# Junction to the first MLP product of a diffusion block: weight splits one step ahead of token sums, weight rows in freed pages, early pairs interleaved

## The chip, the cores and the metric

One core of a Trainium2 chip runs one transformer-like block over 1024 tokens of 1024 channels. The metric is the device time of one execution in microseconds (us), the median of three runs. Engines: PE is TensorE (matmuls; PEld its weight loads), DVE is VectorE, ACT is ScalarE, POOL is GpSimd, SP issues the DMA transfers. Work runs on an engine in the order of its own instruction list; engines wait for each other by semaphores.

## The reference

The part around the change: the residual stream x (1024 tokens) gets its mixing branch, is normalised, scaled and shifted, and goes through a squared-ReLU MLP with D_FF = 4096.

```
x = x + gt1 * branch_merge(...)            # ends in "merged @ w_out", 1024x1024
x = x + gt2 * sq_relu_mlp(modulate(rms_norm(x, g_mlp), sh2, sc2), w1, w2)

def sq_relu_mlp(h, w1, w2):
    return jnp.square(jax.nn.relu(h @ w1)) @ w2
```

gt2 is a vector that a product of the conditioning vector with a 1024x6144 matrix gives.

## The kernel before

**Number format.** A float32 operand is split into a high part (a ScalarE copy to fp32r, a 32-bit format in which PE multiplies in one pass) and a low part (a VectorE subtraction, source minus high part). Both stand in `split` (L98), so nearly every split has line L98. A product then takes three passes: high x high, high x low, low x high. One product of the first MLP multiplication is twelve matmuls of 128x128 by 128x512 (four contraction tiles, three passes), in `mm` (L958).

**Seven products in place of eight.** h @ w1 is cut into 16 `Pair`s n. A pair covers 256 columns of w1 (two arrays of 128x1024 that a weight load brings) and both halves of the contraction and of the tokens, as 2x2 blocks. Strassen-Winograd sums give it seven products: p1 (a11 b11), p2 (a12 b21, added in the same PSUM bank A), p6 (s2 t2, bank B), p5 (s1 t1, bank C), p7 (s3 t3, added in B), p4 (a22 t4, added in B) and p3 (s4 b22, added in C). Weight sums s1 to s4 are made per pair (`sums13`, `sums24`, `s12`, `s34`); token sums t1 to t4 once, for four contraction tiles k. Products that add to one bank have VectorE or ScalarE reading the bank between them: p1 is copied (L967) before p2 adds to A, `p6` is read (L977) before p7 adds to B, p7 is read (L986, L987) before p4 adds to B.

**What comes before.** The projection `out_mm` (L859) makes merged @ w_out in two column halves dh, eight token tiles i each. Two tiles share one PSUM tile of two banks, and the second waits until VectorE has read the first (L893). `norm_tile` normalises a token tile when its second half is done: a square with accumulation on ScalarE (L217), a square root (L211), reciprocal and scaling on VectorE (L212, L813, gives xn[i]). The first four tiles are transposed and modulated in `norm_half0`; the last four in `norm_half1(k)`, k = 0 to 3, which is the junction. `gv.reduce()` makes gt2's row with fp32 matmuls against a vector of ones (L296), read by VectorE (L297).

**One step k of the junction in before.** PE transposes eight 128x128 blocks (L819); ScalarE evacuates them with scale and shift (L823) into b12 and b22; GpSimd makes t3 = b22 - b12 (L842), VectorE t1 = b12 - b11 (L843) and t2 = b22 - t1 (L844), GpSimd t4 = b21 - t2 (L845). Then b22, (t1, t2) and (t3, t4) are split, each by a ScalarE copy and a VectorE subtraction. Behind that `early_top` loads a11 and a12 of pair k+1 into one of four 4 KB work buffers (`wr_tile`) and splits them; p1 and p2 of pairs 0 to 3 are computed between the steps. p6(0) then needs t2 of all k.

**What sets the order.** PE, DVE and ACT are under a manual schedule here: their lists have the order of the code. Before that, in the projection, a scheduler places instructions by priority, and fills a wait of PE with matmuls of the next tile. SP and GpSimd follow the same program. Tiles are taken from pools with a fixed number of slots (24 pages of 4 KB in `pg`, 17 in `yp`, four work buffers); a tile that takes a used slot waits for the slot's last readers.

Of the kernel before, what the change touches and what calls it, by code (L numbers as in the profile page):

```python
# [24 lines left out]
P = 128  # L25
# [6 lines left out]
HB = 512  # L32
# [18 lines left out]
def block_kernel(es: ExitStack, tc: tile.TileContext, a, out):  # L51
# [27 lines left out]
    def page(shape, dt=F32, pool=None, tag="s"):  # L79
        return (pool or pg).tile(shape, dt, tag=tag, name=nm("pg"))  # L80
# [10 lines left out]
    def wr_tile():  # L91
        return wp.tile([P, 1024], F32, tag="wr", name=nm("wr"))
# [654 lines left out]
    with tc.tile_pool(name="yp", bufs=17, reuse_waits="tile") as yp:  # L747
# [89 lines left out]
        def norm_half1(k):  # L837
# [7 lines left out]
            G.tensor_tensor(t34[:, 1], b21, t12[:, 1], ALU.subtract)  # L845
            t = page([P, 2, HB], F32R)
# [52 lines left out]
        gv.reduce()  # L899
# [6 lines left out]
        class Pair:  # L906
# [7 lines left out]

            def early_top(self, new):

                r = wr_tile()
                dma(r, a["w1"][2 * self.n])
                self.put(r, ("a11", "a12"), new([P, 2 * HB], F32R), new([P, 2 * HB], F32R))
# [261 lines left out]
        with tc.manual_schedule(engines={mybir.EngineType.PE, mybir.EngineType.DVE, mybir.EngineType.Activation}):  # L1181
            pr[0].p1()
            norm_half1(0)
            pr[1].early_top(page)
            pr[0].p2()
            pr[1].p1()
            norm_half1(1)
            pr[2].early_top(page)
            pr[1].p2()
            pr[2].p1()  # L1190
            norm_half1(2)
            pr[3].early_top(ypage)
            pr[2].p2()
            pr[3].p1(ypage)
            norm_half1(3)
            pr[3].p2()
            pr[1].load()
            pr[1].sums13()
            for n in range(NP):
                c, nx, early = pr[n], pr[n + 1] if n + 1 < NP else None, n < NE  # L1200
                if not early:
                    c.p1()
                if n > NE:
                    pr[n - 1].out4()
                c.p6()
# [5 lines left out]
                if nx:  # L1211
                    nx.s12()
                else:
                    c.f2 = page([P, T])
                    mlp2.begin()
                c.p7()
                if early:
                    if n + 1 == NE:
                        nx.top()
                    else:  # L1220
                        nx.s34()
                        nx.last()
                    c.p4()
                    c.p3()
                    c.out4()
                    if n + 1 == NE:
                        c.out3()
                else:
                    c.p2()
                    if nx:  # L1230
                        nx.top()
                    c.p3()
                    c.out3()
# [120 lines left out]
```

## Time and profile before

| | us |
|---|---|
| median of 3 runs (lowest, highest) | 1449.17 (1448.98, 1449.18) |
| profiled execution | 1448.78 |
| its span, first to last instruction | 1447.0 |
| PE busy | 1385.9 |
| DVE busy | 1045.1 |
| ACT busy | 605.3 |
| start of p1(0), and of p5(0) behind p6(0), on PE | 776.98, 829.8 |

The profiled execution takes 1.8 us more than its span and lies 0.39 us under the median. PE is the engine whose work fills the span; the other engines matter where PE waits for them. Times on the axis below count from the span's start. The mean granted clock of the span is 0.992 of full speed.

### The profile page before, as it was taken

To read this page: it belongs to the slowest core of one execution; us is meant where nothing else is said; L and a number is where in the kernel's file an instruction comes from. 1 tells how busy PE (TensorE), PEld (TensorE's weight loads), DVE (VectorE), ACT (ScalarE), POOL (GpSimd) and SP (SyncE) were. 2 spreads that over 40 slices of the span, in tenths; PEclk is the share of its full clock that TensorE was granted. 3 is DMA by queue.
4 is the path that set the end of the run, shared out by engine and by line. 5 is a ranking of instruction groups with operands and counts; after the bars stand their busy time and mean duration, and the time that the engine had idled before them with its cause. 6 is when DMAs were issued, how large, how long until landed. Compare 5 with 4: busy or idle time off the path is not lost. (4 is left out here: it accounts for less than half of the span.)

```text
span 1447.0 us, 16245 instructions
## 1 busy us (share of the span) xinstructions
PE 1385.9 (96%) x6352; PEld 1128.9 (78%) x6352; DVE 1045.1 (72%) x1254; ACT 605.3 (42%) x747; POOL 13.0 (1%) x14
## 2 busy tenths in 40 slices
PE   4999999999999999999997799999999999999996
PEld 3888888778888878788875577888887888888885
DVE  7664647789888987844746676666664987969958
ACT  7452337654765577412134422222222544333412
POOL 0000000000000000000000200000000000000000
PEclk9999999999999999999999899999999999999998
DMA  8532712342234225547712142333326562340332
GB/s 331 191 117 68 273 38 73 120 146 84 90 121 148 74 86 177 167 143 246 268 73 102 57 147 102 116 117 117 117 73 219 217 212 72 122 147 1 111 137 102
DMA packets 64556, 192.57 MB, mean 133 GB/s; under 512 B 7203, under 2 KB 7611, under 8 KB 64479
## 3 DMA queue, kind: packets, MB, share of 16 engines
q1 hardware_dynamic: 64479, 191.53, 38.2%
q8 instruction: 50, 0.82, 0.2%
q14 instruction: 27, 0.22, 0.0%
HBM read 154.27 MB, written 37.23 MB: 132 GB/s over the span
## 5 line engine op out<-in xcount | busy, mean ns | idle before, releaser
L321 PE MATMUL mm<-pg,wh 128*128 128x512 f32 x1120 | 308.4, 396 | 0.5 <-DVE pg L98 0.5
L321 PEld LDWEIGHTS mm<-pg,wh 128*128 128x128 f32 x1120 | 204.6, 189 | 43.7 <-DVE pg L98 1.0
L958 PE MATMUL bk<-pg,wh 128*128 128x512 f32 x720 | 225.9, 395 | 1.9 <-DVE wr L297 1.1
L321 PE MATMUL mm<-pg,wl 128*128 128x512 f32 x560 | 175.4, 394 | 0.0
L958 PEld LDWEIGHTS bk<-pg,wh 128*128 128x128 f32 x720 | 135.0, 188 | 34.5 <-DVE wr L297 2.1
L958 PE MATMUL bk<-pg,wl 128*128 128x512 f32 x360 | 141.6, 393 | 0.0
L98 DVE TENSOR_TENSOR wl<-wr,wh 128x1024 fp32r<-128x1024 f32 (+2 forms) x73 | 81.5, 1119 | 76.6 <-ACT wh L98 76.5
L98 ACT ACTIVATE wh<-wr 128x1024 fp32r<-128x1024 f32 (+2 forms) x73 | 71.0, 975 | 147.9 <-PE mm L321 67.0
L321 PEld LDWEIGHTS mm<-pg,wl 128*128 128x128 f32 x560 | 105.4, 188 | 24.3
L98 ACT ACTIVATE wh<-pg 128x1024 fp32r<-128x1024 f32 (+1 forms) x52 | 52.4, 1027 | 141.0 <-PE bk L958 52.7
L98 ACT ACTIVATE pg<-pg 128x1024 fp32r<-128x1024 f32 (+4 forms) x90 | 76.3, 878 | 44.2 <-DMA pg<-act_d 12.6
L859 PE MATMUL mm<-pg,pg 128*128 128x512 f32 x384 | 91.9, 397 | 0.0
L958 PE MATMUL bk<-pg,pg 128*128 128x512 f32 x264 | 71.1, 419 | 19.7 <-ACT pg L98 15.1
L98 DVE TENSOR_TENSOR pg<-pg,pg 128x1024 fp32r<-128x1024 f32 (+4 forms) x79 | 73.8, 969 | 18.0 <-ACT pg L98 17.9
L859 PEld LDWEIGHTS mm<-pg,pg 128*128 128x128 f32 x384 | 71.0, 188 | 17.8 <-DVE g L893 2.2
L958 PEld LDWEIGHTS bk<-pg,wl 128*128 128x128 f32 x360 | 67.6, 188 | 15.9
L958 PEld LDWEIGHTS bk<-pg,pg 128*128 128x128 f32 x264 | 51.9, 201 | 35.9 <-ACT pg L98 19.0
L98 DVE TENSOR_TENSOR wl<-pg,wh 128x1024 fp32r<-128x1024 f32 (+1 forms) x52 | 60.2, 1178 | 22.9 <-ACT wh L98 22.9
L1094 PE MATMUL mm<-pg,pg 128*128 128x512 f32 x240 | 74.1, 390 | 0.0
L776 PE MATMUL mm<-pg,wh 128*128 128x512 f32 x256 | 70.0, 394 | 1.7 <-ACT pg L98 1.7
L1108 DVE TENSOR_TENSOR pg<-pg,mm 128x1024 f32<-128x1024 f32 x34 | 41.0, 1218 | 39.4 <-PE mm L1094 38.3
L1094 PE MATMUL mm<-pg 128*128 128x512 f32 x164 | 64.1, 391 | 0.0
(281 smaller groups left out, 2457.2 us busy)
## 6 DMA issues: line engine op xcount, KB each, us to landing
wr<-in_win SPq DMA_DIRECT2D x36, 512.0 KB, 4.4
wr<-in_w SPq DMA_DIRECT2D x35, 512.0 KB, 3.5
pg<-act_d SPq DMA_DIRECT2D x70, 256.0 KB, 4.9
pg<-in_wm SPq DMA_DIRECT2D x32, 512.0 KB, 8.2
wr<-in_wm SPq DMA_DIRECT2D x32, 512.0 KB, 3.8
act_d<-pg SPq DMA_DIRECT2D x32, 512.0 KB, 3.0
pg<-in_w SPq DMA_DIRECT2D x56, 256.0 KB, 5.4
pg<-in_x SPq DMA_DIRECT2D x16, 512.0 KB, 8.2
```

Of the source, the lines that this page charges most:

```text
L98: return S.activation(hi, src, AF.Copy), V.tensor_tensor(lo, src, f32(hi), ALU.subtract)
L321: PE.matmul(ps[:, h * HB:(h + 1) * HB], l[:, k, :], r[:, h * HB:(h + 1) * HB], start=k == 0 and i == 0, stop=k == KT - 1 and i == 2)
L776: PE.matmul(ps[:, h * HB:(h + 1) * HB], l[:, k, :], r[:, h * HB:(h + 1) * HB], start=k == 0 and i == 0, stop=k == KT - 1 and i == 2)
L859: PE.matmul(ps, l, r, start=k == 0 and j == 0, stop=k == KT - 1 and j == 2)
L958: PE.matmul(ps, l, r, start=first and k == 0 and i == 0, stop=k == 3 and i == 2, skip_group_check=not first)
L1094: PE.matmul(t[j], l, r, start=u not in self.ON and k == 0 and n == 0, stop=k == len(op) - 1 and n == 2, skip_group_check=u in self.ON)
L1108: V.tensor_tensor(t, t, ps, ALU.subtract if u in self.SUB else ALU.add)
```

## The change

1. `gv.reduce()` moves from behind the whole projection to between its two halves.
2. `early_top` is cut in two: `early_load` loads the upper weight rows of a pair into a page of `pg` (before: a work buffer), `early_top` splits them. The load and split of pair 1 come ahead of p1(0); those of pairs 2 and 3 come between the token sums and the splits of steps 0 and 1.
3. `norm_half1` is cut into `half1_sums` (transposes, evacuation, t1 to t4) and `half1_split` (the splits).
4. In pairs 0 to 2, p6 of the next pair stands between p7 and p4; in pair 3, the top split of pair 4 comes ahead of p7 and p1 of pair 4 stands between p7 and p4.

```diff
@@ -834,7 +834,7 @@
                     split(hf[k][:, j], t[:, 0], t[:, 1])
                     tb[("b11", "b21")[j]][k] = (t[:, 0], t[:, 1])
 
-        def norm_half1(k):
+        def half1_sums(k):
             g, t12, t34 = ypage([P, 2, HB]), *(wr_tile().rearrange("p (a b) -> p a b", b=HB) for _ in range(2))
             for j in range(2):
                 norm_block(k + 4 * j, 1, g[:, j], False, bank())
@@ -843,6 +843,9 @@
             V.tensor_tensor(t12[:, 0], b12, b11, ALU.subtract)
             V.tensor_tensor(t12[:, 1], b22, t12[:, 0], ALU.subtract)
             G.tensor_tensor(t34[:, 1], b21, t12[:, 1], ALU.subtract)
+            return b22, t12, t34
+
+        def half1_split(k, b22, t12, t34):
             t = page([P, 2, HB], F32R)
             split(b22, t[:, 0], t[:, 1])
             tb["b22"][k] = (t[:, 0], t[:, 1])
@@ -896,7 +899,8 @@
                     norm_tile(i)
                     if i == 3:
                         norm_half0()
-        gv.reduce()
+            if dh == 0:
+                gv.reduce()
         gt2 = const.tile([P, D], F32, tag="gt", name="gt2")
         dma(gt2, gt_d[1].partition_broadcast(P))
 
@@ -912,11 +916,13 @@
                 for j, r in enumerate(self.r):
                     dma(r, a["w1"][2 * self.n + j])
 
+            def early_load(self):
+
+                self.r0 = page([P, 2 * HB])
+                dma(self.r0, a["w1"][2 * self.n])
+
             def early_top(self, new):
-
-                r = wr_tile()
-                dma(r, a["w1"][2 * self.n])
-                self.put(r, ("a11", "a12"), new([P, 2 * HB], F32R), new([P, 2 * HB], F32R))
+                self.put(self.r0, ("a11", "a12"), new([P, 2 * HB], F32R), new([P, 2 * HB], F32R))
 
             def put(self, src, names, hi, lo):
                 split(src, hi, lo)
@@ -1179,30 +1185,37 @@
             pr[0].last()
         psum_pool("banks", 8)
         with tc.manual_schedule(engines={mybir.EngineType.PE, mybir.EngineType.DVE, mybir.EngineType.Activation}):
+            pr[1].early_load()
+            pr[1].early_top(page)
             pr[0].p1()
-            norm_half1(0)
-            pr[1].early_top(page)
+            h1 = half1_sums(0)
+            pr[2].early_load()
+            pr[2].early_top(page)
+            half1_split(0, *h1)
             pr[0].p2()
             pr[1].p1()
-            norm_half1(1)
-            pr[2].early_top(page)
+            h1 = half1_sums(1)
+            pr[3].early_load()
+            pr[3].early_top(ypage)
+            half1_split(1, *h1)
             pr[1].p2()
             pr[2].p1()
-            norm_half1(2)
-            pr[3].early_top(ypage)
+            h1 = half1_sums(2)
+            half1_split(2, *h1)
             pr[2].p2()
             pr[3].p1(ypage)
-            norm_half1(3)
+            h1 = half1_sums(3)
+            pr[1].load()
+            half1_split(3, *h1)
+            pr[1].sums13()
             pr[3].p2()
-            pr[1].load()
-            pr[1].sums13()
             for n in range(NP):
                 c, nx, early = pr[n], pr[n + 1] if n + 1 < NP else None, n < NE
-                if not early:
+                if n > NE:
                     c.p1()
-                if n > NE:
                     pr[n - 1].out4()
-                c.p6()
+                if n == 0 or not early:
+                    c.p6()
                 if n and early:
                     pr[n - 1].out3()
                 if nx:
@@ -1213,13 +1226,16 @@
                 else:
                     c.f2 = page([P, T])
                     mlp2.begin()
+                if n + 1 == NE:
+                    nx.top()
                 c.p7()
                 if early:
-                    if n + 1 == NE:
-                        nx.top()
-                    else:
+                    if n + 1 < NE:
+                        nx.p6()
                         nx.s34()
                         nx.last()
+                    else:
+                        nx.p1()
                     c.p4()
                     c.p3()
                     c.out4()
```

How this moves the engines' lists, at three places. Lines of the file after are higher by 3 to 6 from L885 on: L859 becomes L862, L958 L964, L967 L973, L971 L977, L977 L983, L986 L992, L987 L993, L993 L999, L1000 L1006, L1004 L1010.

**PE, from the last matmuls of token tile 6 of the second projection half to the first of tile 7.** mm_5793 and mm_5802 are the PSUM tile that both share, smp the gate's bank. Before:

```order
L859 MATMUL mm_5793<-pg_5497,pg_5177 128x512 x2
L859 MATMUL mm_5793<-pg_5497,pg_5178 128x512
L296 MATMUL smp_5866<-gacc,ones 1x512
L859 MATMUL mm_5793<-pg_5304,pg_4761 128x512 x2
L859 MATMUL mm_5793<-pg_5304,pg_4762 128x512
```

After:

```order
L862 MATMUL mm_5802<-pg_5497,pg_5177 128x512 x2
L862 MATMUL mm_5802<-pg_5497,pg_5178 128x512
L862 MATMUL mm_5802<-pg_5304,pg_4761 128x512 x2
L862 MATMUL mm_5802<-pg_5304,pg_4762 128x512
L862 MATMUL mm_5802<-pg_5339,pg_4771 128x512 x2
```

The L296 matmul between the tiles is gone; in the list after the two of them stand ahead of and behind the last tile of the first half.

**ACT, from step 0's evacuation to step 1's.** pg_5922 (after: pg_5928) holds b12, b22 of step 0; wr_5923, wr_5924 (wr_5929, wr_5930) its sums; bk_5907 and bk_5971 (bk_5913, bk_5977) are bank A of pairs 0 and 1. Before:

```order
L823 ACTIVATE pg_5922<-bk_5931,mod 128x512
L98 ACTIVATE pg_5941<-pg_5922 128x512
L98 ACTIVATE pg_5944<-wr_5923 128x1024
L98 ACTIVATE pg_5948<-wr_5924 128x1024
L98 ACTIVATE pg_5954<-wr_5952 128x1024
L971 ACTIVATE pg_5920<-bk_5907 128x512
L967 ACTIVATE pg_5984<-bk_5971 128x512
L823 ACTIVATE pg_5986<-bk_5989,mod 128x512
L823 ACTIVATE pg_5986<-bk_5995,mod 128x512
```

After:

```order
L823 ACTIVATE pg_5928<-bk_5937,mod 128x512
L98 ACTIVATE wh_5890<-pg_5884 128x1024
L98 ACTIVATE wh_5894<-pg_5885 128x1024
L98 ACTIVATE pg_5949<-pg_5947 128x1024
L98 ACTIVATE pg_5953<-pg_5928 128x512
L98 ACTIVATE pg_5956<-wr_5929 128x1024
L98 ACTIVATE pg_5960<-wr_5930 128x1024
L977 ACTIVATE pg_5926<-bk_5913 128x512
L973 ACTIVATE pg_5990<-bk_5977 128x512
L823 ACTIVATE pg_5992<-bk_5995,mod 128x512
```

The copy of weights of pair 1 (pg_5954 from wr_5952) that stood behind step 0's three splits is gone from here (it is made ahead of p1(0)); pair 2's (pg_5949 from pg_5947) stands ahead of them. Behind them the order is as before: relu of p2(0), copy of p1(1), evacuation of step 1.

**DVE, around p7 of pair 2.** bk_6350 (after: bk_6308) is bank B of pair 2, bk_6402 bank B of pair 3 after. Before:

```order
L98 TENSOR_TENSOR wl_6384<-pg_6346,wh_6383 128x1024
L986 TENSOR_TENSOR pg_6387<-pg_6048,bk_6350 128x512
L987 TENSOR_TENSOR pg_6387<-pg_6387,bk_6370 128x512
L98 TENSOR_TENSOR wl_6403<-pg_6347,wh_6402 128x1024
L98 TENSOR_TENSOR pg_6406<-wr_6343,pg_6406 128x512
L993 TENSOR_TENSOR pg_6387<-pg_6048,bk_6350 128x512
L1004 SCALAR_TENSOR_TENSOR pg_6387<-pg_6387 128x1024
```

After:

```order
L98 TENSOR_TENSOR wl_6384<-pg_6361,wh_6383 128x1024
L992 TENSOR_TENSOR pg_6387<-pg_6054,bk_6308 128x512
L993 TENSOR_TENSOR pg_6387<-pg_6387,bk_6370 128x512
L983 TENSOR_TENSOR pg_6403<-pg_6112,bk_6402 128x512
L98 TENSOR_TENSOR wl_6418<-pg_6362,wh_6417 128x1024
L98 TENSOR_TENSOR pg_6421<-wr_6358,pg_6421 128x512
L999 TENSOR_TENSOR pg_6387<-pg_6054,bk_6308 128x512
L1010 SCALAR_TENSOR_TENSOR pg_6387<-pg_6387 128x1024
```

Between the two reads of bank B behind p7 (L992, L993) and the split of s3, s4 stands now the read of the next pair's p6 (L983).

## Rows read from the trace of the kernel before

**Rows 1.** Page, part 1: busy time, share of the span, instructions.

```profile
PE 1385.9 (96%) x6352; PEld 1128.9 (78%) x6352; DVE 1045.1 (72%) x1254; ACT 605.3 (42%) x747; POOL 13.0 (1%) x14
```

**Rows 2.** Waits of PE, whole span: who waited for whom, us in total, times, longest.

```profile
PE bk L958 <- ACT pg L98: 15.1, 3, 7.2
...
PE bk L958 <- DVE pg L986: 3.4, 4, 0.9
...
PE bk L958 <- DVE wr L297: 1.1, 1, 1.1
```

**Rows 3.** One window of the junction: busy us of each engine, PEclk, DMA, GB/s.

```profile
800.00:810.00 10.00, 5.67 (x21) 4.38 (x22) 4.44 (x4) 4.34 (x6) 1.52 (x1) 0.83 0.17 52
```

**Rows 4.** Timeline of PE: start, us, line, op, tiles, count, idle before.

```profile
768.10 1.02 PE L296 MATMUL smp<-gacc,ones 128*1 128x512 f32 x2
...
774.82 1.02 PE L296 MATMUL smp<-gacc,ones 128*1 128x512 f32 x2
...
779.88 1.04 PE L819 MATMUL bk<-ident,pg 128*128 128x128 f32 x8
...
790.98 1.22 PE L958 MATMUL bk<-pg,pg 128*128 128x512 f32 x2 [7.19 <-ACT pg L98]
792.42 3.48 PE L958 MATMUL bk<-pg,pg 128*128 128x512 f32 x10 [0.23 <-DVE pg L98]
...
796.59 3.06 PE L958 MATMUL bk<-pg,pg 128*128 128x512 f32 x12
...
805.06 3.94 PE L958 MATMUL bk<-pg,pg 128*128 128x512 f32 x10 [0.71 <-DVE pg L98]
...
829.21 0.50 PE L958 MATMUL bk<-pg,wh 128*128 128x512 f32 x1 [0.79 <-DVE pg L98]
...
836.26 3.05 PE L958 MATMUL bk<-pg,pg 128*128 128x512 f32 x12 [0.78 <-DVE pg L986]
```

**Rows 5.** Timeline of ScalarE (ACT), junction.

```profile
788.92 2.00 ACT L98 ACTIVATE pg<-wr 128x1024 fp32r<-128x1024 f32 x2 [0.67 <-POOL wr L845]
...
795.94 0.60 ACT L967 ACTIVATE pg<-bk 128x512 f32<-128x512 f32 x1 [4.54 <-PE bk L958]
796.43 1.44 ACT L823 ACTIVATE pg<-bk,mod 128x512 f32<-128x512 f32 x2
...
809.04 0.60 ACT L967 ACTIVATE pg<-bk 128x512 f32<-128x512 f32 x1 [5.00 <-PE bk L958]
```

**Rows 6.** Timeline of VectorE (DVE), junction.

```profile
763.14 0.75 DVE L813 TENSOR_SCALAR pg<-pg,tiny 128x1024 f32<-128x1024 f32 x1
...
772.60 1.42 DVE L813 TENSOR_SCALAR pg<-pg,tiny 128x1024 f32<-128x1024 f32 x2 [1.26 <-PE mm L859]
...
778.09 0.75 DVE L813 TENSOR_SCALAR pg<-pg,tiny 128x1024 f32<-128x1024 f32 x1
...
782.33 2.36 DVE L98 TENSOR_TENSOR wl<-pg,wh 128x1024 fp32r<-128x1024 f32 x2 [0.48 <-ACT wh L98]
...
788.28 4.09 DVE L98 TENSOR_TENSOR pg<-wr,pg 128x1024 fp32r<-128x1024 f32 x3 [0.52 <-ACT pg L98]
...
798.04 1.76 DVE L844 TENSOR_TENSOR wr<-pg,wr 128x512 f32<-128x512 f32 x1
...
827.44 2.98 DVE L98 TENSOR_TENSOR pg<-wr,pg 128x1024 fp32r<-128x1024 f32 x2 [0.52 <-ACT pg L98]
```

**Rows 7.** Timeline of GpSimd (POOL), junction, steps 0 and 1.

```profile
783.99 1.82 POOL L842 TENSOR_TENSOR wr<-pg 128x512 f32<-128x512 f32 x1 [782.68 <-DMA gt<-gt_d]
...
797.96 1.29 POOL L842 TENSOR_TENSOR wr<-pg 128x512 f32<-128x512 f32 x1 [9.07 <-ACT pg L823]
799.87 1.65 POOL L845 TENSOR_TENSOR wr<-pg,wr 128x512 f32<-128x512 f32 x1 [0.62 <-DVE wr L844]
```

**Rows 8.** Page, part 6: DMA issues, KB each, median us to landing.

```profile
wr<-in_w SPq DMA_DIRECT2D x35, 512.0 KB, 3.5
pg<-in_wm SPq DMA_DIRECT2D x32, 512.0 KB, 8.2
```

## The prediction

> **What bounds the kernel now.** Read first the page's busy shares: PE is busy for 96% of the span [rows 1], so only its stops can be won back. The waits of PE come next: in the junction (the products, L958) PE stops 15.1 us in three stops for a ScalarE split, 1.1 us for L297, and four times up to 0.9 us for L986, 3.4 us in all [rows 2]. [...] In the timeline two matmuls behind a stop take 1.22 us and the next ten 3.48 or 3.94 us, 0.34 to 0.39 apart, where twelve take 3.05 us at 836.26, 0.24 apart [rows 4]: about 1.5 us lost per stop. The timelines of ScalarE, VectorE and GpSimd show the chain behind the stops. Below, k is a token-sum step, t12 and t34 its two sums; times are us on the axis of before.
>
> In before one step is a ring: the splits of step k end with the top weight split of pair k+1, only then p1(k+1) runs, then its copy and the transposes, then ScalarE's evacuation (L823), L843, L844, and the splits again. From one copy of p1 to the next it takes 809.04 - 795.94 = 13.1 us [rows 5]. PE has 6.6 us of work in that: two products of 2.85 us (twelve matmuls) and eight transposes, 0.85 us [rows 4].
>
> **The gate reduction.** Its four L296 records move before the second half of the projection. At 768.10 two of them fill a hole of 0.95 us, in which PE waits for VectorE to read the other half of the same PSUM tile; two stand alone at 774.82 [rows 4]. At the new place the first two fill such a hole, where matmuls of the next tile did; the old hole opens. So the projection ends 0.95 + 0.85 = 1.8 us later, near 776.7, and the 1.1 us wait for L297 [rows 2] goes: p1(0) starts at 776.8 instead of 777.0. But the last normalised tile, which took until 778.84, 4.0 us after the projection [rows 4, 6], now ends at 780.65. p1(0) ends at 779.6, so the transposes stop for 1.0 us, and p2(0) starts at 781.3 (780.7 before). This edit alone costs 0.6 us.
>
> **The first weight split ahead.** r0 of pair 1 is loaded into the page of x2[4]. SP issues it when xn[4] is made, 763.9 [rows 6] + 1.8 = 765.7; a 512 KB weight load lands in 3.5 us [rows 8], 769.2. Its split (1.0 us ScalarE, 1.15 us VectorE [rows 5, 6]) stands ahead of the square of tile 6, and also waits for the first matmuls of tile 7, whose slots it takes (769.1 + 1.8 and two matmuls: 771.3). VectorE waits there for PE to free the pages of xn[5] and xn[6], until 772.6 [rows 6] + 1.8 = 774.4, so I cost it at nothing; without that cover it would be 2.2 us. The loads of pairs 2 and 3 stand on SP behind gt2 and the store of x2[7]: issued near 778.3, needed at 786 and 794. Four 512 KB transfers together may take 6 to 7 us; hidden.
>
> So p1(1) needs no wait: 784.1 to 786.95, transposes until 787.8. That removes the stop of 7.2 us [rows 2].
>
> **What is late next.** p2(1) continues in p1(1)'s bank and must wait for ScalarE's copy of it. In ScalarE's new order this copy stands behind the split of t34(0), and that waits for GpSimd. Worked out in order:
> - ScalarE: L823 twice, 781.0 to 782.4 (0.72 each [rows 5]). VectorE from 780.6: pair 0's sums and the split of a22, 0.60 apart; GpSimd's L842 comes in between from 783.1 to 784.4 (1.30 [rows 7]), so the last sum ends at 785.0 and L843 at 785.6.
> - VectorE: two splits of s12, s34 (1.12 apart [rows 6]) to 787.8, L844 to 788.4, pair 2's low half to 789.5. GpSimd's L845 then runs to 790.8, and ScalarE's split of t34 to 791.8.
> - Relu of p2(0), copy of p1(1): 792.9. p2(1) starts at 792.95 (796.6 before [rows 4]): a stop of 5.1 us, with 1.5 us of low clock behind it as after the other stops.
> - Step 1: b22, t12 and t34 low halves hold VectorE until 793.6; L843 to 794.3; L844 beside GpSimd's L842 takes 1.76 [rows 6, 7], to 796.1; pair 3's low half to 797.1; L845 to 798.4; t34 split to 799.4. p1(2) ends near 800.3 because of the low clock, its copy at 801.1: p2(2) follows the transposes at once.
> - Step 2, now without a weight split: L823 to 802.5, L844 to 804.2, L845 to 806.0, t34 to 807.0, copy of p1(3) 808.1; p2(3) from 808.15, a stop of 0.4 us.
> - Step 3: L823 to 809.5, L844 to 811.3, L845 to 813.0, t12's low half 814.2. p6(0)'s eleventh matmul waits for it; in before that is the matmul at 829.21 [rows 4], released by the low half from 827.44 [rows 6].
>
> Gain of the junction: 829.2 - 814.2 = 15.0 us.
>
> One unknown carries most of it: when VectorE and GpSimd wait for each other. L844 beside L842 took 1.76 us instead of 0.69, until 0.55 us after GpSimd's end at 799.25, and three low halves from 788.28 took 4.09 us, as if begun when GpSimd ended at 788.88 [rows 6, 7]. Without such waits step 1 to 3 would each be some 2 us shorter: 6 us more gain. With GpSimd kept out until VectorE's run of splits is over, L845 would come 1.7 us later in each of steps 0 to 2: 5 us less. At 784 GpSimd got in as soon as one split ended (1.82 us for 1.30 [rows 7]); I take that. [...]
>
> **The early pairs.** p4 writes the bank that L986 reads after p7, four stops of 3.4 us [rows 2]; matmuls pitched at 0.23 but lasting 0.39 lose 0.16 more per stop: 4.0 us. p6 of the next pair (for pair 3, p1 of pair 4), 2.85 us, now stands in each hole, longer than L986's 0.7. The new demand: the next pair's s12 split must be ready one p4, p3 earlier. It is started after out3 and two sums; after p3 VectorE needs 0.6 + 1.2 (out3), 1.2 (sums) and 2.1 for the split's halves, 5.1 us, and p5 and p7 give 5.7. Margin 0.6. For pair 4's top split I see a tie. I take the whole 4.0. The L977 of the next pair comes on VectorE ahead of the s34 split, 0.6 us, which p7 needs only 10 us later.
>
> Sum: 15.0 + 4.0 = 19.0 us. The profiled execution took 1448.78 us, a span of 1447.0 and 1.8 around it; 1448.78 - 19.0 = 1429.8, and the median of the runs lies 0.39 above the profiled one: **1430.2**. Behind the early pairs the order is the same and PE is full, so the gain stays to the end.
>
> **The rivals.**
> 1. No stop but that of the last tile: ScalarE keeps up. Then p6(0) would end at 776.7 + 8 x 2.85 + 4 x 0.85 + 1.0 + 2.85 = 806.8 against 829.7, 23 us, and 27 with the pairs: 1422. Against it: the copy's place behind t34. Chance 0.08.
> 2. The ring stays: p2(k+1) waits for its copy in every step, with the low clock each time, and steps stay near 13.1 us. Then only the first step's 3.6 us (796.6 - 792.95) and 4.0 are won: 1441.6. For it: PE's order has the wait in each step. Against it: steps 1 and 2 fit into 8 us by the rows. Chance 0.10. A half-way case, GpSimd kept out (above), gives 1435; it is within my range.
> 3. The interleave only moves the stop, because s12 comes late: 1434.2. Chance 0.08.
> 4. The other side: r0 of pair 1 lands late and holds ScalarE and VectorE ahead of tiles 6 and 7, so that transposes, and everything behind them, move. It costs from 771.3 on, 2.1 us after I expect it; it would be slower than before by over 0.2% if it took some 25 us to land instead of 3.5: 1452. The slowest group of 512 KB loads in the page has a median of 8.2 us [rows 8], which would cost 2.6 us. Chance 0.02.
>
> [...]
>
> **The numbers.** My forecast has 0.69, the rivals 0.28, and 0.03 stay for what I have not seen. The range goes from past the middle between forecast and rival 1 (1425) to past GpSimd kept out (1437): it holds rival 3 and leaves out rivals 1, 2 and 4, which have 0.20. About 0.2% (3 us) is what a measurement of this kernel tells from no change. Faster by more than that: my forecast and rivals 1 to 3, 0.95; within it 0.02; slower 0.03, rival 4 and a third of the unseen.
>
> **What would show it.** L296 between the projection's halves and no wait for L297; no PE wait at p1(1), p1(2), p1(3); one long stop, 4 to 6 us, at the second half of step 1 (p2(1)), waiting for the copy of p1; a short one at the transposes of step 0; no wait of L964 for L992; p5(0) near 815. The prediction fails if stops of 4 us recur in steps 2 and 3, if GpSimd's L845 waits longer than one VectorE split, or if p6 of the next pair waits for a weight split.

## The result, and the profile after

| | before | changed kernel |
|---|---|---|
| median of the runs on one chip (lowest, highest) | 1449.18 (1448.98, 1451.24) | 1430.3 (1429.62, 1431.46) |
| ratio to before, 95% interval | | 0.9867 (0.985 to 0.9884) |
| span of the profiled execution | 1447.0 | 1429.7 |

The kernel is 18.9 us faster; 1430.2 was forecast. On the page's row of PE busy time, with its share of the span, the work is the same but for 2.1 us [rows 1], so what went is waiting:

```profile
PE 1383.8 (97%) x6352; PEld 1128.5 (79%) x6352; DVE 1046.0 (73%) x1254; ACT 605.0 (42%) x747; POOL 14.0 (1%) x14
```

The waits of PE in the changed kernel (who waited for whom, us in total, times, longest), those that belong to the junction and the early pairs:

```profile
PE bk L964 <- ACT pg L973: 5.2, 2, 4.7
...
PE bk L819 <- DVE pg L813: 0.9, 1, 0.9
PE bk L964 <- DVE pg L98: 0.8, 1, 0.8
PE mm L862 <- DVE g L896: 0.8, 1, 0.8
...
PE bk L964 <- DVE wl L98: 0.4, 1, 0.4
```

The 15.1 us behind ScalarE's splits, the 1.1 us for L297 and the four stops behind L986 [rows 2] are gone. 5.2 us for the copy of p1 (L973) have come, 0.9 us at the transposes and 0.8 us in the projection (L896). The 0.4 us for a wl tile were not in the sum. Where they lie is seen in the timeline of PE in the changed kernel:

```profile
770.75 5.85 PE L862 MATMUL mm<-pg,pg 128*128 128x512 f32 x24 [0.78 <-DVE g L896]
...
780.61 0.77 PE L819 MATMUL bk<-ident,pg 128*128 128x128 f32 x5 [0.89 <-DVE pg L813]
...
784.00 2.96 PE L964 MATMUL bk<-pg,pg 128*128 128x512 f32 x12
786.80 1.03 PE L819 MATMUL bk<-ident,pg 128*128 128x128 f32 x8
792.54 7.72 PE L964 MATMUL bk<-pg,pg 128*128 128x512 f32 x24 [4.71 <-ACT pg L973]
800.10 1.03 PE L819 MATMUL bk<-ident,pg 128*128 128x128 f32 x8
800.95 5.78 PE L964 MATMUL bk<-pg,pg 128*128 128x512 f32 x24
...
808.09 3.02 PE L964 MATMUL bk<-pg,pg 128*128 128x512 f32 x12 [0.48 <-ACT pg L973]
...
814.24 0.50 PE L964 MATMUL bk<-pg,wh 128*128 128x512 f32 x1 [0.80 <-DVE pg L98]
```

p1(1) starts at 784.00 with no wait; the stop is now in the middle of step 1, at p2(1), for 4.71 us. Matmuls are twelve to a product; "x24" at 800.95 is p2(2) and p1(3) without a stop between. What PE waits for at 792.54 is read from ScalarE's timeline:

```profile
788.17 1.06 ACT L98 ACTIVATE pg<-wr 128x1024 fp32r<-128x1024 f32 x1 [0.95 <-DVE wr L844]
790.46 1.06 ACT L98 ACTIVATE pg<-wr 128x1024 fp32r<-128x1024 f32 x1 [1.23 <-POOL wr L845]
791.42 0.58 ACT L977 ACTIVATE pg<-bk 128x512 f32<-128x512 f32 x1
791.90 0.59 ACT L973 ACTIVATE pg<-bk 128x512 f32<-128x512 f32 x1
```

and from GpSimd's:

```profile
788.22 2.21 POOL L845 TENSOR_TENSOR wr<-pg,wr 128x512 f32<-128x512 f32 x1 [4.11 <-DVE wr L844]
```

The split of t34 at 790.46 waited 1.23 us for GpSimd's L845, which took 2.21 us, and the copy of p1(1) at 791.90 stands behind that split. Two windows of PE in the changed kernel (their length, PE's busy us and matmuls, granted clock, DMA share, GB/s) show what the stop leaves behind:

```profile
792.50:796.50 4.00, 3.96 (x9) 0.50 0.00 0
796.50:800.10 3.60, 3.60 (x16) 0.97 0.00 0
```

In the first 4 us behind it the granted clock is 0.50, so 24 matmuls take 7.72 us, where 5.78 us do at 800.95, at 1.00. ScalarE's copy of p1(2), which opens step 2, then waits for PE:

```profile
800.30 0.60 ACT L973 ACTIVATE pg<-bk 128x512 f32<-128x512 f32 x1 [0.70 <-PE bk L964]
```

### The profile page after: what moved, and what is told of

Same layout as the page of the kernel before. It is cut to its first block, busy times and chain, and to the rows that moved or that the text cites. A ratio compares the mean times of both kernels' runs of the same rounds, so it can differ in the third digit from the quotient of the medians.

```text
span 1429.7 us, 16245 instructions
## 1 busy us (share of the span) xinstructions
PE 1383.8 (97%) x6352; PEld 1128.5 (79%) x6352; DVE 1046.0 (73%) x1254; ACT 605.0 (42%) x747; POOL 14.0 (1%) x14
## 4 chain that ended last, share of the span: by engine, by line
PE 86%; DVE 5%; ACT 3%; DMA 3%; issue 2%; POOL 0%; SPq 0%; DVEq 0%; POOLq 0%; ACTq 0%
PE mm L321 24%; PE bk L964 19%; PE mm L1100 19%; PE mm L862 6%; PE mm L776 6%; PE mm L1172 3%; PE mm L621 2%; PE smp L596 2%; DMA wr<-in_win 1%; PE mm L686 1%; PE smp L622 1%; PE mm L497 1%; ACT jk L217 1%; DVE l L653 1%; ACT wh L98 1%
## 5 line engine op out<-in xcount | busy, mean ns | idle before, releaser
L964 PE MATMUL bk<-pg,wh 128*128 128x512 f32 x720 | 226.3, 395 | 0.9 <-DVE pg L98 0.8
L964 PEld LDWEIGHTS bk<-pg,wh 128*128 128x128 f32 x720 | 135.1, 188 | 33.5 <-DVE pg L98 1.2
L964 PE MATMUL bk<-pg,wl 128*128 128x512 f32 x360 | 141.9, 394 | 0.4 <-DVE wl L98 0.4
L98 ACT ACTIVATE pg<-pg 128x1024 fp32r<-128x1024 f32 (+4 forms) x93 | 79.3, 884 | 46.5 <-DMA pg<-act_d 13.1
L98 DVE TENSOR_TENSOR pg<-pg,pg 128x1024 fp32r<-128x1024 f32 (+4 forms) x82 | 79.4, 1004 | 18.9 <-ACT pg L98 18.8
L862 PE MATMUL mm<-pg,pg 128*128 128x512 f32 x384 | 92.4, 398 | 0.8 <-DVE g L896 0.8
L862 PEld LDWEIGHTS mm<-pg,pg 128*128 128x128 f32 x384 | 71.0, 188 | 19.6 <-DVE g L896 3.1
L964 PEld LDWEIGHTS bk<-pg,wl 128*128 128x128 f32 x360 | 67.6, 188 | 16.8 <-DVE wl L98 0.8
L964 PE MATMUL bk<-pg,pg 128*128 128x512 f32 x264 | 66.6, 403 | 5.2 <-ACT pg L973 5.2
L964 PEld LDWEIGHTS bk<-pg,pg 128*128 128x128 f32 x264 | 50.7, 193 | 17.6 <-ACT pg L973 5.7
```

Of the source, the lines that this page charges most:

```text
L98: return S.activation(hi, src, AF.Copy), V.tensor_tensor(lo, src, f32(hi), ALU.subtract)
L862: PE.matmul(ps, l, r, start=k == 0 and j == 0, stop=k == KT - 1 and j == 2)
L964: PE.matmul(ps, l, r, start=first and k == 0 and i == 0, stop=k == 3 and i == 2, skip_group_check=not first)
```

## The experiments

**Theory.** PE's stops in before came from the order of ScalarE's and VectorE's work: the weight split of the next pair stood behind the token sums' splits. Putting it ahead gives the junction's gain; what remains is bound by the chain token sums, GpSimd, t34 split, copy of p1. **Rivals.** The freed pages do it, because weights land sooner; the junction and the interleave share one gain; the end of the junction is bound by VectorE alone, so that the stop at p2(1) costs nothing.

The profiled executions come to the projection's first matmul between 678.55 and 681.03 us (680.34 in before, 679.87 after), and what comes ahead of it is the same work in all. So the table counts from that matmul, by PE's timeline of each: the start of p2(0), of p2(1), and of p6(0)'s eleventh matmul. "Stage" is from the start of p7(0) to that of p7(4), 21 products. The kernels ran on several chips, each beside runs of before on the same chip; where two rows come from different chips, their ratios are the better comparison.

| kernel | median us | ratio to before (95%) | p2(0) | p2(1) | p6(0), 11th matmul | stage |
|---|---|---|---|---|---|---|
| before | 1448.8 to 1451.0 | | 100.39 | 116.25 | 148.87 | 62.71 |
| changed | 1430.30 | 0.9867 (0.985–0.9884) | 101.25 | 112.67 | 134.37 | 59.52 |
| changed, again | 1430.90 | 0.9872 (0.9855–0.9888) | 101.28 | 112.69 | 135.22 | 59.54 |
| interleave only | 1446.79 | 0.9979 (0.9969–0.9988) | 100.40 | 117.15 | 150.48 | 59.31 |
| no interleave | 1434.74 | 0.9899 (0.9884–0.9914) | 101.22 | 112.64 | 134.92 | 62.91 |
| splits behind | 1449.05 | 0.9997 (0.9987–1.0008) | 101.21 | 119.17 | 153.08 | 59.48 |
| ring | 1431.54 | 0.9878 (0.9863–0.9893) | 101.23 | 112.61 | 135.10 | 59.55 |
| gate late | 1430.44 | 0.9865 (0.9851–0.9878) | 100.43 | 111.31 | 132.66 | 59.55 |
| top ahead | 1430.36 | 0.9868 (0.9854–0.9883) | 101.23 | 112.62 | 134.79 | 58.88 |
| copy first | 1432.38 | 0.9877 (0.9863–0.989) | 101.23 | 107.82 | 132.67 | 59.53 |
| vector sums | 1427.76 | 0.9849 (0.9836–0.9863) | 101.24 | 110.47 | 130.12 | 59.59 |
| both of these | 1426.00 | 0.9836 (0.982–0.9853) | 101.21 | 107.74 | 128.95 | 59.54 |
| vector sums, gate late | 1424.41 | 0.9813 (0.9797–0.983) | 100.43 | 108.34 | 126.76 | 59.54 |
| the same, top ahead | 1423.26 | 0.982 (0.9805–0.9835) | 100.42 | 108.34 | 126.78 | 58.87 |

**Interleave only.** Before, with the pairs' order of the change.

```diff
-                if not early:
+                if n > NE:
                     c.p1()
-                if n > NE:
                     pr[n - 1].out4()
-                c.p6()
+                if n == 0 or not early:
+                    c.p6()
...
+                if n + 1 == NE:
+                    nx.top()
                 c.p7()
                 if early:
-                    if n + 1 == NE:
-                        nx.top()
-                    else:
+                    if n + 1 < NE:
+                        nx.p6()
                         nx.s34()
                         nx.last()
+                    else:
+                        nx.p1()
```

> The kernel before with the fourth part of the change alone: p6 of the next pair (for pair 3, p1 of pair 4) between p7 and p4. If the four stops at the read of bank B are closed and nothing takes their place, about 4.0 us less than before (1445.2), with the first product of the pairs (p5 of pair 0) near 829.8 as before and no wait of the products for L986. Seen in the changed kernel, p1 of pair 4 takes 0.7 us longer and its follower 0.3, so 3.0 to 3.5 us is likelier. The rival (the interleave only moves the stops to the weight splits of the next pair): 0 to 1.5 us less, and waits of L958 for a split in each of pairs 1 to 3.

3.1 us faster by the medians. The stage is 3.4 us shorter, and the junction of this execution, with the same instructions as in before, took 1.6 us longer. The window of PE behind the second wait of p1, in before:

```profile
804.00:812.00 8.00, 7.29 (x30) 0.79 0.21 66
```

and in the kernel with the interleave only:

```profile
804.00:812.00 8.00, 7.35 (x24) 0.63 0.20 66
```

Behind the same stop of 3.96 us the mean granted clock of this window is lower here (0.63 against 0.79). Thirteen runs of before on this chip lie the same way: the four with a mean clock of 0.992 took 1448.1 to 1449.6 us, the four with 0.988 took 1450.2 to 1450.7, and the five between them 1449.1 to 1451.1. The profiled execution of before, on which the prediction's sum was made, has 0.992: it is one of the shorter ones.

**No interleave.** The changed kernel with the pairs' order of before.

```diff
+                if not early:
+                    c.p1()
                 if n > NE:
-                    c.p1()
                     pr[n - 1].out4()
-                if n == 0 or not early:
-                    c.p6()
+                c.p6()
...
-                if n + 1 == NE:
-                    nx.top()
                 c.p7()
                 if early:
-                    if n + 1 < NE:
-                        nx.p6()
+                    if n + 1 == NE:
+                        nx.top()
+                    else:
                         nx.s34()
                         nx.last()
-                    else:
-                        nx.p1()
```

> The changed kernel without the interleave of the early pairs (their products in the order of before), the junction as changed. Theory A (the two halves of the change add): the four stops of the pair stage come back, 4.05 us between the eleventh matmul of p6(0) and the last product of the early pairs by the two traces, less the 0.9 that pair 4's first product lost to its late top split: 3.2 to 4 us slower than the changed kernel, some 1434, with p6(0)'s eleventh matmul where the changed kernel has it (814.2, within 0.3). Rival B (the run with the interleave alone gained 3.1 of these by letting the stage start 1.5 us later, so part of the gain belongs to the junction): less than 2 us slower, under 1432.5.

The stage is 3.4 us longer, and p6(0) is where the two executions of the changed kernel have it (134.92 between 134.37 and 135.22). The ratios differ by 0.003, some 4 us. Theory A: the two halves of the change add.

**Splits behind.** The changed kernel with load and split of the upper weight rows where before has them; pages, gate and interleave stay.

```diff
-            pr[1].early_load()
-            pr[1].early_top(page)
             pr[0].p1()
             h1 = half1_sums(0)
-            pr[2].early_load()
-            pr[2].early_top(page)
             half1_split(0, *h1)
+            pr[1].early_load()
+            pr[1].early_top(page)
...
```

Steps 1 and 2 are changed likewise for pairs 2 and 3.

> The changed kernel with the load and the split of the upper weight rows of pairs 1 to 3 put back behind the split of the token sums of their step (pages, interleave and gate stay as changed). Theory A (the ring was: weight split late, so p1 late, so its copy late, so the next transposes late): p1(1) to p1(3) wait for their splits again, 3 to 5 us each, the eleventh matmul of p6(0) comes 8 to 13 us later than in the changed kernel, some 1438 to 1444. Rival B (the loads and buffers were the limit, not the order of the splits; early pages alone free it): under 1434, with waits of p1 below 1.5 us each.

PE's timeline in steps 0 and 1 of this kernel:

```profile
792.39 1.22 PE L964 MATMUL bk<-pg,pg 128*128 128x512 f32 x2 [7.80 <-ACT pg L98]
793.84 4.63 PE L964 MATMUL bk<-pg,pg 128*128 128x512 f32 x10 [0.23 <-DVE pg L98]
...
806.54 1.22 PE L964 MATMUL bk<-pg,pg 128*128 128x512 f32 x2 [4.00 <-ACT pg L98]
807.99 4.63 PE L964 MATMUL bk<-pg,pg 128*128 128x512 f32 x10 [0.23 <-DVE pg L98]
```

and ScalarE's in step 0, the split of t34 and behind it that of pair 1's weights:

```profile
790.34 1.06 ACT L98 ACTIVATE pg<-wr 128x1024 fp32r<-128x1024 f32 x1 [0.68 <-POOL wr L845]
791.30 1.04 ACT L98 ACTIVATE pg<-pg 128x1024 fp32r<-128x1024 f32 x1
```

All of the gain is gone: p6(0) is 17.9 to 18.7 us later than in the two executions of the changed kernel, more than theory A gave. The three waits are back, 15.8 us in all, where before has 15.1 [rows 2]. What they leave was not in that expectation: ten matmuls behind each take 4.63 us, at a mean granted clock of 0.54 to 0.59 in the windows of 8 to 10 us around them. The time is that of before, 2.3 us above the interleave alone; p6(0) is 2.6 us later than there. The loads stand later in the code too, but the weight split at 791.30 follows the one ahead of it without a wait, so its place in ScalarE's list holds it and not its load. So the order of the splits is the junction's whole gain; without it the gate and the pages gain nothing. A kernel with the order alone, without pages and gate, was not run; those with one of the two taken back follow (ring, gate late).

**Ring.** The changed kernel with the early rows in the four work buffers.

```diff
-                self.r0 = page([P, 2 * HB])
+                self.r0 = wr_tile()
```

> The changed kernel with the upper weight rows of pairs 1 to 3 loaded into the ring of four buffers that they share with the token sums, as before, and not into freed pages; the order of the splits stays one step ahead. Theory A (both edits are needed: in the ring r0 of pair 2 can only be loaded when the split of pair 0's a22 has read its buffer, near 786, and lands 3.5 us later, so its split, which now stands ahead of that of the token sums, holds ScalarE and VectorE for 3 us in step 0, and again less in step 1): p2(1) 2.5 to 4 us later than in the changed kernel (792.5), p6(0)'s eleventh matmul 2 to 5 us later, total 1432.5 to 1435.5. Rival B (the order alone does it, the pages nothing): total within 1.5 us of the changed kernel in the same call.

Theory A fell. The weights do land later, and ScalarE waits for them (timeline of ScalarE):

```profile
786.83 1.06 ACT L98 ACTIVATE pg<-wr 128x1024 fp32r<-128x1024 f32 x1 [0.67 <-DMA wr<-in_w]
...
790.84 1.06 ACT L98 ACTIVATE pg<-wr 128x1024 fp32r<-128x1024 f32 x1 [1.20 <-POOL wr L845]
...
792.28 0.59 ACT L973 ACTIVATE pg<-bk 128x512 f32<-128x512 f32 x1
...
796.05 1.06 ACT L98 ACTIVATE pg<-wr 128x1024 fp32r<-128x1024 f32 x1 [1.85 <-DMA wr<-in_w]
```

But it then waits 1.20 us for L845, as in the changed kernel, and the copy of p1(1) at 792.28 is as late, with this execution's start 0.44 us later, as the one at 791.90. The wait for the late weights lies under that for GpSimd's sums; the freed pages gain nothing that shows: p6(0) is at 135.10, between the two executions of the changed kernel, and the median 0.6 us above that of the changed kernel on the same chip (rival B).

**Gate late.** The changed kernel with `gv.reduce()` behind the projection, as before.

```diff
-            if dh == 0:
-                gv.reduce()
+        gv.reduce()
         gt2 = const.tile([P, D], F32, tag="gt", name="gt2")
```

> The changed kernel with the gate reduction back behind the projection. As the prediction has it, this part alone costs 0.6 us at the second product: so the projection ends near 774.9 again, p1 of pair 0 starts near 777.0 behind a wait of 1.1 us for L297, the last normalised tile is ready at 778.8 instead of 780.5, the transposes do not stop, and the junction ends 0.4 to 1.7 us earlier than in the changed kernel (1428.6 to 1429.9). The rival (the move pays, because it takes the wait for L297 off PE): 1.1 us slower than the changed kernel (1431.4).

The profile has the move at a loss: p2(0) is 0.8 us earlier without it, p2(1) 1.36 and p6(0) 1.7 to 2.6. The times agree within their intervals, and the median lies 0.5 us above the range expected, so that only the profile tells it here.

**Copy first.** The changed kernel with `half1_split(k)` behind p2(k) and p1(k+1), so that the copies stand ahead of the splits.

```diff
-            half1_split(0, *h1)
             pr[0].p2()
             pr[1].p1()
+            half1_split(0, *h1)
...
```

Steps 1 and 2 likewise.

> The changed kernel, but the splits of steps 0 to 2 stand in the code behind p2 of the pair and p1 of the next, so that ScalarE copies p1 of the next pair before the splits; PE's order stays. The stop of 4.7 us at p2 of pair 1 goes in either theory. Theory A (the chain of VectorE, GpSimd and ScalarE over the steps sets the end, the stop lies only partly on it): PE then waits at later products, most of all p6 of pair 0, and the junction ends 2 to 3.5 us earlier (about 1427.3). Theory B (what is left of the junction's loss is PE's stop and the slow clock behind it): 6 us or more earlier (1424).

PE's timeline in p6(0) of this kernel:

```profile
810.91 0.50 PE L964 MATMUL bk<-pg,wh 128*128 128x512 f32 x1 [3.90 <-ACT pg L98]
812.64 0.80 PE L964 MATMUL bk<-pg,wh 128*128 128x512 f32 x1 [1.23 <-DVE pg L98]
```

Two windows of PE behind that:

```profile
812.00:816.00 4.00, 3.36 (x8) 0.50 0.59 158
816.00:820.00 4.00, 4.00 (x14) 0.70 0.63 227
```

The stop at p2(1) is gone and p6(0) starts 6.6 to 7.5 us earlier, but then waits 3.90 and 1.23 us for t2(3): the chain of the token sums ends the junction, not the copy, and so the last link of the theory falls. Until the eleventh matmul 1.7 us are won against one execution of the changed kernel and 2.6 against the other, near theory A and far from B. They are lost again, since the low clock now falls on products that nothing else would have held up: p7(0) starts as late as in one execution of the changed kernel and 0.9 us later than in the other, and the time, 1432.4, is no better than that of the changed kernel (the intervals overlap), where theory A had 1427.3. Up to p6(0) the stop at p2(1) was worth 1.7 to 2.6 us, not its 4.71; behind it, taking the stop away like this won nothing.

**Vector sums.** The changed kernel with t3 and t4 on VectorE, both behind t1 and t2.

```diff
-            G.tensor_tensor(t34[:, 0], b22, b12, ALU.subtract)
             V.tensor_tensor(t12[:, 0], b12, b11, ALU.subtract)
             V.tensor_tensor(t12[:, 1], b22, t12[:, 0], ALU.subtract)
-            G.tensor_tensor(t34[:, 1], b21, t12[:, 1], ALU.subtract)
+            V.tensor_tensor(t34[:, 0], b22, b12, ALU.subtract)
+            V.tensor_tensor(t34[:, 1], b21, t12[:, 1], ALU.subtract)
```

In this kernel L842 is therefore t1, L843 t2, L844 t3 and L845 t4.

> The changed kernel with t3 and t4 made on VectorE instead of GpSimd: eight more VectorE instructions of 0.60 us, 4.8 us, and no GpSimd work in the junction. If VectorE and GpSimd exclude each other as the prediction took it, 948 falls from 1.78 to 0.69 us, L844 from 1.76 to 0.69 in each step and the low halves of two splits from 2.91 to 2.35 us: VectorE's run over the junction gets 2.5 to 3.5 us shorter, and so does the junction (about 1427.3). If GpSimd runs beside VectorE and its waits are something else, VectorE's run gets longer by most of 4.8 us: 1433 to 1435.

The timelines of GpSimd and VectorE in step 0 of the changed kernel:

```profile
782.50 1.61 POOL L842 TENSOR_TENSOR wr<-pg 128x512 f32<-128x512 f32 x1 [781.20 <-DMA x_d<-pg]
782.87 1.78 DVE L948 TENSOR_TENSOR pg<-wr,pg 128x512 f32<-128x512 f32 x1
...
788.06 2.91 DVE L98 TENSOR_TENSOR pg<-pg,pg 128x1024 fp32r<-128x1024 f32 x2
```

and VectorE's of this one:

```profile
782.10 0.69 DVE L948 TENSOR_TENSOR pg<-wr,pg 128x512 f32<-128x512 f32 x1
782.71 0.68 DVE L842 TENSOR_TENSOR wr<-pg,pg 128x512 f32<-128x512 f32 x1
...
787.39 1.82 DVE L98 TENSOR_TENSOR pg<-pg,pg 128x1024 fp32r<-128x1024 f32 x2
```

L948 takes 0.69 us instead of the 1.78 beside GpSimd's L842, two low halves 1.82 instead of 2.91: two ops more on VectorE per step, and yet a shorter chain. p6(0) is 4.2 to 5.1 us earlier, more than the 2.5 to 3.5 expected. The ratios differ by 0.2% (0.9849 and 0.9867), some 2.6 us, but their intervals overlap: the gain is the profile's.

**Both of these.** Copy first and vector sums together, by the two diffs above.

> The changed kernel with all four token sums on VectorE and the split of the token sums written behind the copies of p2(k) and p1(k+1). Theory A (two separate waits: GpSimd's sums held the split of t3 and t4, and this split held the copy; the one with VectorE's sums already takes most of the second's gain): no stop at p2(1) to p2(3) above 0.5 us, p6(0) waits for t2(3) as with the copies ahead alone but 1 to 2 us shorter, since VectorE's chain is shorter: eleventh matmul at 807.5 to 810, total 1427 to 1429. Rival B (the gains add, 5.0 and 1.6): eleventh matmul before 808 and total below 1426. Rival C (the long stop at the start of p6(0) leaves the low clock where nothing hides it, as with the copies ahead alone): total 1428.5 to 1430.5 although the eleventh matmul is no later than with VectorE's sums alone.

No p2(k) stops, and p6(0) waits 1.23 and 1.36 us; the eleventh matmul is 1.2 us earlier than with vector sums alone, but p7(0) 0.5 us later (133.88 against 133.42), by the low clock: behind these waits two matmuls take 1.06 us, as where copy first has 0.50, and 0.62 at 814.90 (rival C's mechanism). The median, 1426.0, is 1.8 us lower than with vector sums alone and below the totals of A and C; the intervals overlap, and the profiled executions do not show a gain. Which of the two is faster stays open.

**Vector sums, gate late, top ahead.** Three edits on the changed kernel: the diffs of vector sums and gate late, and

```diff
+                if n + 1 == NE:
+                    nx.top()
                 if nx:
                     nx.s12()
                 else:
                     ...
-                if n + 1 == NE:
-                    nx.top()
                 c.p7()
```

> The changed kernel with three edits: all token sums on VectorE, the gate's reduction back behind the projection's second half, and the top split of pair 4 ahead of its s12 split. By the profiles: 5.0 at the sums (as measured with the first edit alone, 1427.8), 0 to 1.2 at the gate's reduction, and 0.6 to 0.9 at p1(4), which waits for its weights in every run with the interleave. Theory A (they add): 1425.5 to 1427, p1(4) in 2.8 us, p2(0) at about 780.8. Rival B (s12 of pair 4 is late next, so the stop only moves to p5 or p6 of pair 4; and the gate's reduction costs the wait of the junction again): 1427.3 to 1428.5, no better than the sums alone.

1423.3 us is under theory A's range: 26.5 us faster than before on the same chip, 4.5 under the median of vector sums alone on another, where the gate and the top split add to 0.6 to 2.1 by the expectation. It is the fastest of all kernels here, with the one without the top split's edit. The runs with the top split alone and without it tell where the rest is from.

**Top ahead.** The last of the three edits alone.

> The changed kernel with the top split of pair 4 started ahead of its s12 split and not behind it. Theory A (the tie at p1(4) was lost by 0.7 us, and the buffers of the two splits are the only other thing that changes place): p1(4) in 2.8 instead of 3.5 us, no wait for the low half of a wl tile, and the last product of the stage 0.6 to 1.0 us earlier; the time some 0.7 us lower, which is under what the runs can tell. Rival B (pair 4's s12 split is then late for its p6): p1(4) in 2.8 us, and the same 0.7 us lost at pair 4's first products behind it.

p1(4) takes 2.81 instead of 3.47 us, and the stage is 0.65 us shorter: theory A.

**Changed, again.** No edit.

> The changed kernel itself, on the same chip as the two others: 1429.5 to 1431.5, p6(0)'s eleventh matmul 813.5 to 814.9, p1(4) 3.5 us.

The timelines of PE and ScalarE:

```profile
791.24 8.54 PE L964 MATMUL bk<-pg,pg 128*128 128x512 f32 x24 [4.69 <-ACT pg L973]
799.82 0.60 ACT L973 ACTIVATE pg<-bk 128x512 f32<-128x512 f32 x1 [1.52 <-PE bk L964]
```

The stop is the same (4.69 us), but the 24 matmuls behind it take 8.54 us, 0.8 more than in the first profiled execution: the granted clock is 0.50 from 791.20 to 795.20 as there, then 0.77 until 799.60, where it was 0.97 there. The copy of p1(2) waits 0.8 us longer for PE, and p6(0) is 0.85 us later. The other executions with this stop lie between in the same order: the 24 matmuls took 8.19 us in top ahead, 8.31 in no interleave and 8.49 in ring, the copy waited 1.17, 1.30 and 1.43 us, and p6(0) is at 134.79, 134.92 and 135.10. Less this wait, p6(0) is at 133.62 to 133.70 in all five executions. So it is the time of these 24 matmuls that sets apart the p6(0) of these kernels, and not their edits.

**Vector sums, gate late.** Without the top split's edit.

> The changed kernel with all token sums on VectorE and the gate's reduction back behind the projection's second half; pair 4's top split as in the changed kernel. It splits the 4.5 us by which the version with the top split moved too was faster than the one with VectorE's sums alone (1423.3 against 1427.8), of which the top split is 0.7. Theory A (with the reduction behind the projection the stop at p2(1) shrinks from 2.5 to 1.2 us, and the granted clock then stays at 1.00, where it was 0.55 and 0.91 behind the longer stop): from the start of p1(0) to p6(0)'s eleventh matmul 30.0 to 30.5 us, against 33.6 with VectorE's sums alone, granted clock 1.00 behind the stop, total 1423.5 to 1425. Rival B (the gate is worth no more than the 1.2 us seen with GpSimd's sums in place, and the rest of the 4.5 is the spread between runs): 32 to 33 us, total 1425.5 to 1427.

Theory A: 30.08 us from p1(0) to the eleventh matmul, 33.57 with vector sums alone; the intervals of the two ratios lie apart. PE's stop at p2(1) with vector sums alone:

```profile
789.58 7.25 PE L964 MATMUL bk<-pg,pg 128*128 128x512 f32 x24 [2.52 <-ACT pg L973]
```

and the windows of PE behind it:

```profile
789.00:792.00 3.00, 2.42 (x6) 0.55 0.00 0
792.00:796.00 4.00, 4.00 (x18) 0.91 0.00 0
```

The same stop with the gate late too (lines of this kernel are lower by one):

```profile
789.37 5.84 PE L963 MATMUL bk<-pg,pg 128*128 128x512 f32 x24 [1.19 <-ACT pg L972]
```

and its windows:

```profile
789.00:792.00 3.00, 2.63 (x11) 1.00 0.00 0
792.00:796.00 4.00, 4.00 (x23) 1.00 0.00 0
```

The reduction behind the projection lets the last tile, and with it VectorE's chain, come earlier than PE's own work: the stop shrinks from 2.52 to 1.19 us, and behind the shorter one the granted clock stays at 1.00. That is 3.4 us at p6(0): 2.1 until p2(1), 1.2 behind it.

## Why the prediction was right, point by point

- **The gate reduction.** Place and times as forecast: a hole of 0.78 us in the projection again, no wait for L297, a stop of 0.89 us at the transposes, p2(0) 0.85 us later. That this edit alone costs 0.6 us was too little: the run with it undone is 1.7 to 2.6 us earlier at p6(0), since the late last tile also starts VectorE's chain late. The sum contained that, since the chain was worked out from 780.65; the price put on the edit did not.
- **The first weight split ahead.** It ran on ScalarE at 771.52 (771.3 forecast) and cost nothing visible. The loads of the three pairs landed in 3.4 to 6.3 us, where 3.5 stood for the first and 6 to 7 for four transfers together. p1(1) needs no wait, and with the splits put back behind the token sums p6(0) is 17.9 to 18.7 us later and all of the gain is gone: shown. That the rows lie in a freed page is not needed (ring).
- **What is late next.** The stop at p2(1), its length (5.1 forecast, 4.71) and its chain were as worked out, op by op: copy of p1(1) behind the split of t34 behind L845. p2(1) started at 792.54 (792.95), p2(3) at 808.09 (808.15), p6(0)'s eleventh matmul at 814.24 (814.2). GpSimd's L845 ended at 790.43 (790.8), as if it had got in after one of VectorE's splits, as taken. The low clock (0.83 in a window of before [rows 3], 0.50 in the first 4 us here) cost 1.9 us behind it in one execution and 2.8 in another, where 1.5 stood. It did not lie under ScalarE's work: ScalarE was done with step 1 at 799.60 and then waited 0.70 us for PE's p1(2) (1.52 in the second execution), and p6(0) moved by as much (changed, again). The steps of the prediction had p1(2) end late, at 800.3, and so contained it for the first execution.
- **The unknown.** Waits between VectorE and GpSimd: without GpSimd's sums 4.2 to 5.1 us more are won at p6(0), where 6 stood. The run does not price the waits alone: it also swaps GpSimd's own 1.3 us per sum for 0.6 on VectorE and puts the sums in another order. L948 took 1.78 us beside L842 and 0.69 without it; what makes one of them wait for the other is not shown.
- **The early pairs.** The mechanism was right and the term was too large: 4.0 stood, the stage is 3.2 us shorter. The four stops are gone, but the tie at pair 4's top split was lost, by 0.7 us at p1(4), which comes back with the split ahead of s12. A further 0.26 us stand ahead of p7(4), at 877.12. The profile names no releaser, but p7 must wait until VectorE has read p6(4) from the bank (L983), and this read, from 876.30 to 876.98, ends a run of VectorE's work that has no pause since 871.49. That it is the cause is read from this order and not tested. With both losses the 3.2 us of the stage make 4.1, the 4.0 of the sum.
- **The sum.** From the projection's start to p6(0) 14.5 us were won (13.7 in the second execution) where 15.0 stood, in the stage 3.2 where 4.0 stood, and 0.8 were lost evenly over the products behind it, so "the gain stays to the end" was not quite so. The terms were 2.1 us too large together: 16.9 us. That the changed kernel's execution was 0.47 us ahead at the projection's start makes the 17.3 us by which the spans differ. The runs' medians differ by 18.9. Of that 1.6 us more, 0.4 is what the profiled execution of before lies below its median, which the sum had; 1.2 is what that of after lies above its own, as the highest of its four runs. So the mechanism was right and its terms a little large, and that the forecast of 1430.2 met the median to 0.1 us is luck.
- **The rivals.** No case of the rivals showed. The ring of before (rival 2) is what the kernel with the splits behind does; a stop moved by the interleave (rival 3) happened once, at p1(4); r0 of pair 1 was in time (rival 4). The price of rival 4 has a slip: by its own times a landing of 25 us costs 790.7 - 771.3 = 19.4 us, which gives 1449.6, the time of before; 1452 takes some 27 us.

## What to carry to other kernels

When PE stops for a split, look at the order of the engines that make it: here one split per step moved ahead of work that waits for another engine anyway was worth the junction's whole gain, and where its data lies was worth nothing. Price a stop by what it leaves as well: a stop of 1.19 us left the granted clock at 1.00, stops of 2.52 to 4.71 us cost 1.5 to 2.8 us more behind them (24 matmuls took 7.25 to 8.54 us instead of 5.8). Between the stops of 2.52 and 1.19 us, 1.3 us less waiting was worth 2.7 us on PE. And a stop that is taken away may only move the low clock to where nothing hides it (copy first). Take small ops off GpSimd where they stand in one chain with VectorE's; here the chain got shorter although VectorE got the work (p6(0) 4.2 to 5.1 us earlier).

## What was not expected of the hardware

- The low clock lasted differently behind the same stop: 24 matmuls took 7.72 and 8.54 us behind 4.7 us in two executions of one kernel (granted clock 0.97 and 0.77 behind the first 4 us, which had 0.50), and 8.19 to 8.49 in three others with the same stop; ten matmuls took 3.94, 4.41 and 4.63 us behind 3.96 to 4.00 us in three kernels (mean granted clock 0.79, 0.63 and 0.57 in a window of 8 us there). No run shows what sets its length.
- From p7(4) to the last of these products PE took 224.8 and 224.9 us in before and interleave only, 225.0 in ring, 225.5 to 226.0 in all others, spread evenly at some 0.03 us per four products. The order there is the same in all. I have no run that tells the cause; it stays open.
